# Two MLPs on one core: M1 units moved from ahead of P1 and behind P3 to between P7 and P4, and eight modulation columns read a unit later

## The chip, the cores and the metric

The kernel runs on one core of one Trainium2 chip. The metric is the time of one execution on the device, in microseconds (us), from the first to the last instruction with what the device adds around it. TensorE (PE) does the matmuls, VectorE (DVE) and ScalarE (ACT) the elementwise work. DMAs are issued from three queues: SP's, ScalarE's and GpSimd's (POOL); those on POOL's queue can add what they bring to what lies in the tile (accumulating DMAs).

## The reference

Two decoder layers on 512 tokens of width 1024, all in float32. Each layer has a mixer (pooling in layer 0, a gated unit in layer 1) and an MLP of width 4096; both are modulated by a condition vector. The change touches the MLPs and the modulation:

```python
for i in range(2):
    mod = silu(c) @ ada_w[i] + ada_b[i]              # 6 x 1024 numbers
    sh1, sc1, g1, sh2, sc2, g2 = split(mod, 6)
    h = rmsnorm(x, norm_mix_g[i]) * (1 + sc1) + sh1
    x = x + g1 * mixer(h)                            # pool_mixer, then sgu_mixer
    h = rmsnorm(x, norm_mlp_g[i]) * (1 + sc2) + sh2
    x = x + g2 * (square(relu(h @ mlp_w1[i])) @ mlp_w2[i])
return rmsnorm(x, final_g)
```

## The kernel before

**Precision.** Each operand of a large product is split into a high and a low part: ScalarE writes the high part (`wh`, `oh`; line 176 for weights, line 637 for activations), then VectorE subtracts it from the original and writes the low part (`wl`, `ol`; lines 177 and 638). A product is then three matmuls (`mm3`): low x high, high x low, high x high (lines 187, 188, 190).

**The MLP** (`mlp`) is cut into units that TensorE runs one after the other, in the order of the list `units`. M1 is the first product (h times `mlp_w1`), M2 the second (times `mlp_w2`); the 4096 inner features are cut into four chunks of 1024, with eight feature blocks in each.

- An *f unit* is one block of M1 done directly: 48 matmuls of 256 columns. Layer 0 does chunks 0 and 1 of M1 so (f0 to f7 of chunk 0, f10 to f17 here for chunk 1), layer 1 chunk 0.
- An *s unit* (c, j, m) is one of the seven products (m = 1, 5, 6, 3, 7, 2, 4) of a Strassen-like scheme for half j of chunk c of M1: 24 matmuls of 256 columns. Its finished blocks of `g` are written by VectorE and ScalarE (lines 823 to 831).
- A *p unit* P1, P2, P5, P6, P3, P7, P4 is one of the seven products of such a scheme for one chunk of M2: 24 matmuls of 512 columns into two PSUM banks `pm`. P1, P6, P7 and P4 add into one pair of banks, P5 and P3 and then P2 into another, and after each p unit the pair is added to or subtracted from `y` by VectorE (line 941), or copied by ScalarE the first time (line 944). So P4's first matmul waits until line 941 has read P7's result out of the same pair.
- A *q unit* does the last chunk of M2 directly.

In chunk c of M2 the M1 units of chunk c + 1 are mixed in: `lead` of them ahead of P1, then after P1, P2, P5, P6, P3, P7, P4 as many as `step` says. The order on TensorE is the order written down here. What runs on VectorE, ScalarE, SP and POOL is put in order by a scheduler when the program is built, from the order in which `prep` (operands of later units), `extra` and `run` are called; each engine then keeps to its order.

**Weights.** `raw4` loads 512 KB of weights into one of three buffers (tag `w4`) by a DMA on SP's queue. `wh` and `wl` have five buffers each. P1's weights `bt` (1 MB) have one buffer, which P1, P5, P6 and P4 use in turn, with accumulating DMAs on POOL's queue in between; the next chunk's `bt` is loaded when P4's has been split.

**Modulation.** The layers' modulation vectors are computed on VectorE beside the matmuls: a column of `ada_w` (512 KB, tile `ada`) is loaded on SP's queue (`ada_load`, line 205), then multiplied by the spread condition vector and summed (`ada_tile`, line 215). The two columns of a pair end in `finish_mods` (line 195). In layer 0's MLP `COLUMNS[q]` is the number of the unit in whose turn column q is taken up. Columns 0 to 7 use the three `w4` buffers and are loaded and read in the same turn (`modulation`); columns 8 to 17 have a buffer of their own (`get_gb`) and are read some turns after their load (`modulation_late`), where a copy of one element on ScalarE (line 214), from the latest weight tile, keeps the scheduler from reading earlier.

Of the kernel before, what the change touches and what calls it, by code (L numbers as in the profile page):

```python
# [76 lines left out]
COLUMNS = (0, 1, 2, 3, 5, 9, 12, 14, 19, 22, 25, 28, 31, 34, 37, 40, 44, 48, 57, 58, 58, 58, 58, 58)  # L77
# [4 lines left out]
def decoder_kernel(ctx: ExitStack, tc: tile.TileContext, xtok, vecs, rows, fgrow, ada0, adag, ada1, pool_w, w1s, w1, w1f, w1b, w2, w2e, w_v, w_u, w_o, wsT, lnp, bs, out):  # L82
# [120 lines left out]
    def ada_load(src, get):  # L203
        r = get()
        nc.sync.dma_start(r, src)
        return r

    def ada_tile(i, t, r, late=False):

        b, j = divmod(t, 2)  # L210
        if j == 0:
            pmv[i, b] = sm.tile([P, 2], F32, name="pmv", tag="pmv")
        if late:
            A.activation(pmv[i, b][:, j : j + 1], f32(latest[0])[:, 0:1], AF.Copy)
        V.scalar_tensor_tensor(r, r, 1.0, cb, ALU.mult, ALU.mult, accum_out=pmv[i, b][:, j : j + 1])  # L215
        if j == 1:
            finish_mods(i, b, pmv.pop((i, b)))
# [57 lines left out]
    with (  # L275
# [14 lines left out]
        m = band.rearrange("p n g w -> p (n g) w")  # L290
        G.affine_select(out=m, in_=m, compare_op=ALU.is_ge, fill=0.0, base=0, pattern=[[0, 8], [1, W]], channel_multiplier=-1)
        for g in range(4):
            m = band[:, :, g]
# [297 lines left out]
        for k in range(KD):  # L591
# [16 lines left out]
            fs = [slice(P * f, P * f + P) for f in range(SWEEP)]  # L608
# [18 lines left out]
    ORDER = (1, 5, 6, 3, 7, 2, 4)  # L627
# [15 lines left out]
    def mlp(i, first, extra, last, ending):  # L643
# [3 lines left out]
        with (  # L647
# [339 lines left out]
            units = [("f", (0, f)) for f in range(done, 8)]  # L987
            for c in range(3):
                if c + 1 < FROM[i]:
                    fs, lead, step = [("f", (c + 1, f)) for f in range(8)], 3, (1,) * 7  # L990
                else:
                    fs, lead, step = [("s", (c + 1, j, m)) for j in range(2) for m in ORDER], 3, (1, 2, 3, 2, 2, 1, 0)
                units += fs[0:lead]
                fs = fs[lead:]
                for m, n in zip(ORDER2, step):
                    units.append(("p", (c, m)))
                    units += fs[0:n]
                    fs = fs[n:]
# [97 lines left out]
    def column_at(q):  # L1096
        return (0, 40 + q) if q < 8 else (1, q - 8)

    def modulation(q, get):

        return lambda: ada_tile(*column_at(q), ada_load(ada1[q], get))

    def modulation_late(q, n, get, wait=4):

        r = []
        return [(n, lambda: r.append(ada_load(ada1[q], get))), (n + wait, lambda: ada_tile(*column_at(q), r[0], True))]
# [3 lines left out]
        normed(0, 1, 0)  # L1110


    ex = [(n, modulation(q, get4)) for q, n in enumerate(COLUMNS[:8])]
    for q in range(8, 18):
        ex += modulation_late(q, COLUMNS[q], get_gb, min(4, COLUMNS[q + 1] - COLUMNS[q]))
    ex += [(52, lambda: spread_cols(mods[0][:, c_g(1, 0) : c_g(1, 0) + KD], "gain0"))]
    ex += [(n, modulation(q, get4)) for q, n in enumerate(COLUMNS) if q >= 18]
    mlp(0, first0, ex, gated, ending0)


# [6 lines left out]
    with (  # L1127
# [40 lines left out]
        ex = [modulation(q, get4) for q in range(24, 32)]  # L1168
# [102 lines left out]
    ex = [x for q in range(8) for x in modulation_late(48 + q, 8 + 5 * q, late_gb if q == 0 else get_gb)]  # L1271
    ex += [(58, lambda: spread_cols(mods[1][:, c_g(1, 0) : c_g(1, 0) + KD], "gain1"))]
    mlp(1, first1, ex, last1, lambda: None)


# [78 lines left out]
```

## Time and profile before

| what | value |
|---|---|
| median of 3 runs | 867.54 us (865.52, 867.54, 867.67) |
| profiled execution, its own time | 868.02 us |
| its span, first to last instruction | 866.3 us |
| mean granted TensorE clock | 0.990 |
| TensorE busy | 846.1 us, 98% of the span |
| VectorE busy | 686.6 us, 79% |
| ScalarE busy | 482.5 us, 56% |
| POOL busy | 65.3 us, 8% |

In the span, layer 0's MLP lies between about 90 and 390 us and layer 1's between about 540 and 862 us. A line of a timeline has start and duration in us, the engine, the line of the kernel, the operation, the tiles (out<-in, without buffer numbers), the shapes, and in brackets the idle time of the engine before it with what ended it. "SPq" and "POOLq" are the engines' queues where a DMA is issued.

### The profile page before, as it was taken

The numbers are of one execution on the slowest core, as the hardware profiler recorded it, in microseconds if no ns is written. First come the engines' busy times: TensorE is split into PE (matmuls) and PEld (weight loads), VectorE is DVE, ScalarE is ACT, GpSimd is POOL, SyncE is SP. The second block draws the span as 40 slices with busy tenths as digits, with TensorE's granted clock in tenths as the row PEclk, the third lists the DMA queues.
The fourth block names the chain that finished last, engine by engine and source line by source line (L and its number), as shares of the span: only waits on it lengthen the run. The fifth ranks groups of instructions, "written<-read, shape, count | busy, mean of one in ns | idle before, by whom it ended". The sixth has DMA issues, their size and how long they took to land.

```text
span 866.3 us, 13047 instructions
## 1 busy us (share of the span) xinstructions
PE 846.1 (98%) x5116; PEld 752.4 (87%) x5116; DVE 686.6 (79%) x914; ACT 482.5 (56%) x708; POOL 65.3 (8%) x89
## 2 busy tenths in 40 slices
PE   8999989999999998999999999999999999999996
PEld 7778989989998997888888888999999898999885
DVE  6889697677889888857698866777888988887755
ACT  5286845556656467237433325667766666666521
POOL 3000000010101010010020001000101000010001
PEclk9999989999999999999999999999999999999999
DMA  9969965677879784735755644957789788767302
GB/s 354 417 227 319 327 211 165 193 198 198 200 257 198 234 233 186 254 111 184 242 181 180 198 138 172 333 142 200 153 263 202 252 219 240 203 131 259 122 25 97
DMA packets 43218, 182.34 MB, mean 210 GB/s; under 512 B 4859, under 2 KB 5011, under 8 KB 36118
## 3 DMA queue, kind: packets, MB, share of 16 engines
q1 hardware_dynamic: 35282, 137.72, 44.1%
q0 software_dynamic: 7440, 41.43, 23.8%
q10 hardware_dynamic: 436, 2.37, 0.8%
q8 instruction: 40, 0.66, 0.3%
q14 instruction: 20, 0.16, 0.1%
HBM read 175.19 MB, written 6.30 MB: 210 GB/s over the span
## 4 chain that ended last, share of the span: by engine, by line
PE 72%; DVE 11%; DMA 10%; ACT 4%; issue 3%; SPq 0%; POOLq 0%; POOL 0%; DVEq 0%; ACTq 0%
PE po L187 13%; PE po L190 13%; PE po L188 13%; PE pm L187 10%; PE pm L190 10%; PE pm L188 10%; DMA ada<-in_ada 4%; DVE wl L177 3%; DMA wh<-in_ada 2%; DVE ada L402 1%; ACT wh L176 1%; DVE ada L215 1%; DMA wl<-in_ada 1%; DVE y L941 1%; DMA raw<-in_w1b 1%
## 5 line engine op out<-in xcount | busy, mean ns | idle before, releaser
L187 PE MATMUL po<-hb,wl 128*128 128x256 f32 (+1 forms) x697 | 206.3, 296 | 3.1 <-DVE wl L177 3.0
L188 PE MATMUL po<-hb,wh 128*128 128x256 f32 (+1 forms) x696 | 205.4, 295 | 0.0
L190 PE MATMUL po<-hb,wh 128*128 128x256 f32 (+1 forms) x696 | 205.2, 295 | 0.0
L176 ACT ACTIVATE wh<-raw 128x1024 fp32r<-128x1024 f32 (+1 forms) x122 | 125.8, 1037 | 103.7 <-PE pm L190 36.5
L177 DVE TENSOR_TENSOR wl<-raw,wh 128x1024 fp32r<-128x1024 f32 (+1 forms) x122 | 145.9, 1200 | 44.5 <-ACT wh L176 44.2
L187 PEld LDWEIGHTS po<-hb,wl 128*128 128x128 f32 x697 | 132.1, 190 | 7.9 <-DVE wl L177 3.7
L187 PE MATMUL pm<-wh,ol 128*128 128x512 f32 x336 | 132.6, 395 | 4.5 <-ACT qh L637 3.2
L190 PEld LDWEIGHTS po<-hb,wh 128*128 128x128 f32 x696 | 132.0, 190 | 4.1
L188 PEld LDWEIGHTS po<-hb,wh 128*128 128x128 f32 x696 | 132.1, 190 | 3.9
L190 PE MATMUL pm<-wh,oh 128*128 128x512 f32 (+1 forms) x375 | 132.1, 369 | 0.0
L188 PE MATMUL pm<-wl,oh 128*128 128x512 f32 x336 | 132.0, 393 | 0.0
L215 DVE SCALAR_TENSOR_TENSOR ada<-ada,cb 128x1024 f32<-128x1024 f32 x56 | 68.1, 1219 | 31.3 <-DMA ada<-in_ada 31.0
L190 PEld LDWEIGHTS pm<-wh,oh 128*128 128x128 f32 x375 | 71.1, 190 | 15.2
L187 PEld LDWEIGHTS pm<-wh,ol 128*128 128x128 f32 x336 | 63.8, 190 | 17.1 <-ACT qh L637 3.3
L188 PEld LDWEIGHTS pm<-wl,oh 128*128 128x128 f32 x336 | 63.8, 190 | 11.9
L187 PE MATMUL po<-as,wl 128*128 128x256 f32 x240 | 66.3, 276 | 0.0
L188 PE MATMUL po<-as,wh 128*128 128x256 f32 x240 | 66.3, 276 | 0.0
L190 PE MATMUL po<-as,wh 128*128 128x256 f32 x240 | 66.3, 276 | 0.0
L177 DVE TENSOR_TENSOR wl<-bt,wh 128x1024 fp32r<-128x1024 f32 x48 | 58.3, 1220 | 6.7 <-ACT wh L176 6.5
L177 DVE TENSOR_TENSOR wl<-b,wh 128x1024 fp32r<-128x1024 f32 x36 | 43.7, 1222 | 22.6 <-ACT wh L176 22.5
L176 ACT ACTIVATE wh<-bt 128x1024 fp32r<-128x1024 f32 x48 | 50.2, 1056 | 10.0 <-PE pm L190 2.9
L1050 ACT ACTIVATE tmp<-x 128x512 f32<-128x512 f32 (+1 forms) x25 | 15.3, 611 | 63.9 <-DVE x L1046 57.9
(220 smaller groups left out, 1556.2 us busy)
## 6 DMA issues: line engine op xcount, KB each, us to landing
ada<-in_ada SPq DMA_DIRECT2D x72, 512.0 KB, 4.7
raw<-in_w1b SPq DMA_DIRECT2D x40, 512.0 KB, 5.2
b<-in_w SPq DMA_DIRECT2D x18, 1024.0 KB, 6.0
bt<-in_w POOLq DMA_DIRECT2D x16, 1024.0 KB, 8.5
raw<-in_w1b POOLq DMA_DIRECT2D x20, 512.0 KB, 5.8
raw<-in_w2e SPq DMA_DIRECT2D x16, 512.0 KB, 3.5
bt<-in_w SPq DMA_DIRECT2D x6, 1024.0 KB, 6.5
b<-in_w POOLq DMA_DIRECT2D x6, 1024.0 KB, 9.2
```

The lines of the kernel that those rows point to most:

```text
L176: A.activation(h[:, c], r[:, c], AF.Copy)
L177: V.tensor_tensor(l[:, c], r[:, c], f32(h[:, c]), ALU.subtract)
L187: T.matmul(o[:, c], wl, mh[:, c], start=first and not c.start, stop=False, **kw)
L188: T.matmul(o, wh, ml, start=False, stop=False, **kw)
L190: T.matmul(o[:, c], wh, mh[:, c], start=False, stop=last and c.stop is None, **kw)
L215: V.scalar_tensor_tensor(r, r, 1.0, cb, ALU.mult, ALU.mult, accum_out=pmv[i, b][:, j : j + 1])
L402: V.scalar_tensor_tensor(r, r, 1.0, cb, ALU.mult, ALU.mult, accum_out=out)
L941: V.tensor_tensor(yt, yt, banks[hf], ALU.subtract if minus else ALU.add)
L1050: A.activation(tmp, xt, AF.Square, scale=D**-0.5, accum_out=s[:, len(cs) : len(cs) + 1])
```

## The change

`step` for the directly done chunk gives up the f unit between P3 and P7, so that f17 runs between P7 and P4. For the chunks with s units, `lead` goes from 3 to 2, so P1, P2, P5, P6, P3 and P7 come one s unit earlier, and `step` gains one s unit between P7 and P4 (two instead of one). Columns 0 to 7 are taken with `modulation_late` and a wait of one unit.

```diff
                 if c + 1 < FROM[i]:
-                    fs, lead, step = [("f", (c + 1, f)) for f in range(8)], 3, (1,) * 7
+                    fs, lead, step = [("f", (c + 1, f)) for f in range(8)], 3, (1, 1, 1, 1, 0, 1, 0)
                 else:
-                    fs, lead, step = [("s", (c + 1, j, m)) for j in range(2) for m in ORDER], 3, (1, 2, 3, 2, 2, 1, 0)
+                    fs, lead, step = [("s", (c + 1, j, m)) for j in range(2) for m in ORDER], 2, (1, 2, 3, 2, 2, 2, 0)
...
-    ex = [(n, modulation(q, get4)) for q, n in enumerate(COLUMNS[:8])]
+    ex = [x for q in range(8) for x in modulation_late(q, COLUMNS[q], get4, 1)]
```

The units by number (layer 0) around the first places: before, P3 was unit 12, f17 13, P7 14, P4 15; now P3 is 12, P7 13, f17 14, P4 15. In chunk 1, P1 goes from 19 to 18 and P7 from 34 to 33; P4 stays at 36. All three s-unit chunk changes of layer 1 and both of layer 0 shift alike.

VectorE, at the beginning of layer 0's MLP, before. The `ada` rows of line 215 are the first three column reads, `wl_948` is the low half of f11's weights, `wl_1015` that of f12, `u` and `ol` belong to p units, `as` to the s units:

```order
L721 TENSOR_TENSOR ada_955<-xf_109 128x1024
L215 SCALAR_TENSOR_TENSOR ada_951,pmv_953<-ada_951,cb_101 128x1024
L722 TENSOR_TENSOR xf_109<-xf_109 128x4x256
L723 TENSOR_TENSOR xf_109<-xf_109 128x4x256
L215 SCALAR_TENSOR_TENSOR ada_1018,pmv_953<-ada_1018,cb_101 128x1024
L195 TENSOR_TENSOR mods0_89<-pmv_953,vec_78 128x2
L879 TENSOR_TENSOR u_1427<-g_917 128x1024
L215 SCALAR_TENSOR_TENSOR ada_1092,pmv_1094<-ada_1092,cb_101 128x1024
L177 TENSOR_TENSOR wl_948<-raw_945,wh_947 128x1024
L177 TENSOR_TENSOR wl_1015<-raw_1012,wh_1014 128x1024
```

And now (f12's low half is `wl_1013`):

```order
L721 TENSOR_TENSOR ada_953<-xf_109 128x1024
L722 TENSOR_TENSOR xf_109<-xf_109 128x4x256
L723 TENSOR_TENSOR xf_109<-xf_109 128x4x256
L879 TENSOR_TENSOR u_1432<-g_917 128x1024
L177 TENSOR_TENSOR wl_948<-raw_945,wh_947 128x1024
L177 TENSOR_TENSOR wl_1013<-raw_1010,wh_1012 128x1024
L638 TENSOR_TENSOR as_1022<-xf_109,as_1022 128x1024
L215 SCALAR_TENSOR_TENSOR ada_951,pmv_1016<-ada_951,cb_101 128x1024
L638 TENSOR_TENSOR ol_1080<-g_917,oh_1079 128x1024
L177 TENSOR_TENSOR wl_1084<-bt_1077,wh_1083 128x1024
L177 TENSOR_TENSOR wl_1088<-bt_1077,wh_1087 128x1024
```

The low halves of f11 and f12 moved from behind three column reads to ahead of the first; `wl_1084` and `wl_1088` are P1's.

VectorE around P7's drain (line 941) in chunk 2 of layer 0, before. `wl_3269` and `wl_3273` are P4's weight halves, `g_2988` of line 826 a block of M1, `wl_3336` a weight tile of the q units:

```order
L830 TENSOR_TENSOR g_2988<-g_2988,po_2989 128x2x256
L177 TENSOR_TENSOR wl_3269<-bt_2595,wh_3268 128x1024
L826 TENSOR_TENSOR g_2988<-g_2988,po_3236 128x2x256
L177 TENSOR_TENSOR wl_3273<-bt_2595,wh_3272 128x1024
L177 TENSOR_TENSOR wl_3336<-raw_3333,wh_3335 128x1024
L941 TENSOR_TENSOR y_1255<-y_1255,pm_2719 128x512
L941 TENSOR_TENSOR y_1255<-y_1255,pm_2720 128x512
```

And now, with the bank pair `pm_2691`, `pm_2692`:

```order
L830 TENSOR_TENSOR g_2996<-g_2996,po_2997 128x2x256
L177 TENSOR_TENSOR wl_3276<-bt_2597,wh_3275 128x1024
L177 TENSOR_TENSOR wl_3280<-bt_2597,wh_3279 128x1024
L941 TENSOR_TENSOR y_1259<-y_1259,pm_2691 128x512
L941 TENSOR_TENSOR y_1259<-y_1259,pm_2692 128x512
L177 TENSOR_TENSOR wl_3344<-raw_3341,wh_3343 128x1024
L638 TENSOR_TENSOR ql_3366<-g_2624,qh_3365 128x512
L826 TENSOR_TENSOR g_2996<-g_2996,po_3283 128x2x256
```

The drain moved ahead of the M1 block of line 826 and of the q units' split.

VectorE between two column reads of chunk 1 of layer 0, before:

```order
L215 SCALAR_TENSOR_TENSOR ada_2053,pmv_2050<-ada_2053,cb_101 128x1024
L787 TENSOR_TENSOR raw_1965<-raw_1965,raw_2048 128x1024
L195 TENSOR_TENSOR mods1_90<-pmv_2050,vec_78 128x2
L638 TENSOR_TENSOR ol_2301<-s_2029,oh_2300 128x1024
L199 SCALAR_TENSOR_TENSOR scl10_93<-mods1_90,vec_78 128x1
L177 TENSOR_TENSOR wl_2202<-raw_1965,wh_2201 128x1024
L177 TENSOR_TENSOR wl_2234<-raw_2048,wh_2233 128x1024
L215 SCALAR_TENSOR_TENSOR ada_2172,pmv_2265<-ada_2172,cb_101 128x1024
```

And now:

```order
L215 SCALAR_TENSOR_TENSOR ada_2061,pmv_2058<-ada_2061,cb_101 128x1024
L787 TENSOR_TENSOR raw_1946<-raw_1946,raw_2056 128x1024
L195 TENSOR_TENSOR mods1_90<-pmv_2058,vec_78 128x2
L199 SCALAR_TENSOR_TENSOR scl10_93<-mods1_90,vec_78 128x1
L177 TENSOR_TENSOR wl_2210<-raw_1946,wh_2209 128x1024
L177 TENSOR_TENSOR wl_2276<-b_2268,wh_2275 128x1024
L177 TENSOR_TENSOR wl_2280<-b_2268,wh_2279 128x1024
L941 TENSOR_TENSOR y_1259<-y_1259,pm_1907 128x512
L941 TENSOR_TENSOR y_1259<-y_1259,pm_1908 128x512
L177 TENSOR_TENSOR wl_2284<-raw_2056,wh_2283 128x1024
L215 SCALAR_TENSOR_TENSOR ada_2180,pmv_2289<-ada_2180,cb_101 128x1024
```

Between the two reads there stood six rows, and now nine.

## The prediction

> **What bounds the kernel now.** I read the page first, then the list of waits of TensorE, then a table by stretches of time, and the timeline of each engine around the few places that stood out. The page's span, its busy line of TensorE and the shares of the chain that ended last:
>
> ```profile
> span 866.3 us, 13047 instructions
> PE 846.1 (98%) x5116; PEld 752.4 (87%) x5116; DVE 686.6 (79%) x914; ACT 482.5 (56%) x708; POOL 65.3 (8%) x89
> PE 72%; DVE 11%; DMA 10%; ACT 4%; issue 3%; SPq 0%; POOLq 0%; POOL 0%; DVEq 0%; ACTq 0%
> ```
>
> TensorE is busy for 846.1 of 866.3 us, so a change of order can return only the rest, and whatever TensorE spends at a low clock. The waits of TensorE (total, times, longest):
>
> ```profile
> PE pm L187 <- ACT qh L637: 3.2, 1, 3.2
> PE po L187 <- DVE wl L177: 3.0, 1, 3.0
> PE pm L187 <- DVE y L941: 1.4, 2, 1.0
> ```
>
> These lie in the first MLP. By stretches (length, busy us and instructions of PE, PEld, DVE, ACT, POOL, then granted clock, DMA share, GB/s):
>
> ```profile
> 110.00:120.00 10.00, 7.84 (x45) 7.84 (x46) 10.00 (x12) 3.32 (x5) 0.00 (x0) 0.66 0.64 215
> 340.00:350.00 10.00, 6.84 (x23) 5.46 (x23) 8.33 (x10) 7.55 (x13) 0.00 (x0) 0.66 0.42 128
> 350.00:360.00 10.00, 10.00 (x46) 8.24 (x45) 9.82 (x19) 1.89 (x3) 0.00 (x0) 1.00 0.75 258
> ...
> 540.00:850.00 310.00, 310.00 (x2089) 284.50 (x2089) 246.69 (x270) 193.29 (x255) 24.41 (x31) 1.00 0.70 194
> ```
>
> The second MLP (540 to 850) has no idle time of TensorE to win, only some to lose. In the first, two stretches show a gap and a granted clock of 0.66. So the forecast is a list of four gaps, each with what follows it.
>
> **The first chunk: columns read a unit later.** TensorE stops after f10 and waits for the weights of f11:
>
> ```profile
> 108.90 0.28 PE L190 MATMUL po<-hb,wh 128*128 128x256 f32 x1
> 112.16 0.58 PE L187 MATMUL po<-hb,wl 128*128 128x256 f32 x1 [2.99 <-DVE wl L177]
> 112.54 0.41 PE L188 MATMUL po<-hb,wh 128*128 128x256 f32 x1
> ...
> 118.05 0.28 PE L187 MATMUL po<-hb,wl 128*128 128x256 f32 x1
> 118.17 0.28 PE L188 MATMUL po<-hb,wh 128*128 128x256 f32 x1
> ```
>
> Idle: 2.99 us. Then the steps are 0.21 us instead of 0.113 us until 118.05: 27 matmuls take 5.89 us where 27 x 0.1133 = 3.06 would do, 2.83 lost. Together 5.82 us. What VectorE did meanwhile, and when ScalarE had the high half of f11 (first row) and f12 (second) ready:
>
> ```profile
> 101.06 1.10 ACT L176 ACTIVATE wh<-raw 128x1024 fp32r<-128x1024 f32 x1
> ...
> 102.52 1.10 ACT L176 ACTIVATE wh<-raw 128x1024 fp32r<-128x1024 f32 x1
> ...
> 104.80 1.23 DVE L215 SCALAR_TENSOR_TENSOR ada<-ada,cb 128x1024 f32<-128x1024 f32 x1 [2.40 <-DMA ada<-in_ada]
> ...
> 106.15 1.22 DVE L879 TENSOR_TENSOR u<-g 128x1024 f32<-128x1024 f32 x1
> 109.74 1.23 DVE L215 SCALAR_TENSOR_TENSOR ada<-ada,cb 128x1024 f32<-128x1024 f32 x1 [2.37 <-DMA ada<-in_ada]
> ...
> 110.89 2.36 DVE L177 TENSOR_TENSOR wl<-raw,wh 128x1024 fp32r<-128x1024 f32 x2
> ```
>
> VectorE is in order; it stood before three column reads whose data had not landed, with the low halves of f11 and f12 (wl_948, wl_1015) queued behind. In the changed order both stand ahead of the first column read and wait for ScalarE alone: 102.2 + 1.15 and 103.6 + 1.15, so ready near 103.4 and 104.8, for use at 109.2 and 114.6. The cover is 5.8 us. Next in the queue are as_1022, one column read, ol_1080 and P1's two weight halves, five at 1.15 us, done near 110.6, for P1 at 109.2 + 2 x 5.44 = 120.1 (an f unit is 48 matmuls x 0.1133). So this gap goes whole: 5.82 us. Each of the eight columns holds its buffer of three a unit longer, so SP's next weight load waits longer; the 9.5 us left at P1 is what hides that. The eight added copies of one column on ScalarE cost 0.2 us each, by the rows of those that later columns have already:
>
> ```profile
> L214 ACT ACTIVATE pmv<-wh x18: 183/202/205, 216.0 to 742.6; 128x1 f32<-128x1 f32 x18
> ```
>
> 1.6 us in all, on an engine that is busy for 3.32 of the 10 us from 110: taken as nothing. Without that cover they would cost at most 1.6; the lower bound is nothing, since a copy takes no work off any engine.
>
> **The moved M1 units.** The three other gaps are all in front of the same unit, P4. P4 adds into the two PSUM banks that P7 has just filled, so its first matmul waits until VectorE's line 941 (the drain into y) has read them. The waits' list names ScalarE for the last gap, but the rows show the drain ending just before it:
>
> ```profile
> 186.50 0.47 PE L187 MATMUL pm<-wh,ol 128*128 128x512 f32 x1 [0.40 <-DVE y L941]
> 264.19 0.47 PE L187 MATMUL pm<-wh,ol 128*128 128x512 f32 x1 [0.98 <-DVE y L941]
> 344.18 0.77 PE L187 MATMUL pm<-wh,ol 128*128 128x512 f32 x1 [3.16 <-ACT qh L637]
> 344.74 0.63 PE L188 MATMUL pm<-wl,oh 128*128 128x512 f32 x1
> ...
> 350.21 0.40 PE L190 MATMUL pm<-wh,oh 128*128 128x512 f32 x1
> 350.44 0.40 PE L187 MATMUL pm<-wh,ol 128*128 128x512 f32 x1
> ```
>
> Idle 0.40, 0.98 and 3.16 us. After the last, 14 matmuls from 344.18 to 350.21 take 6.03 us instead of 14 x 0.23 = 3.22 (0.23 is the step after 350.21), 2.81 lost. The end of P7 in chunk 2, and VectorE until its drain:
>
> ```profile
> 337.88 0.40 PE L190 MATMUL pm<-wh,oh 128*128 128x256 f32 x2
> ...
> 338.83 0.68 DVE L826 TENSOR_TENSOR g<-g,po 128x512 f32<-128x512 f32 x1
> 340.09 1.22 DVE L177 TENSOR_TENSOR wl<-bt,wh 128x1024 fp32r<-128x1024 f32 x1 [0.58 <-ACT wh L176]
> 342.21 1.23 DVE L177 TENSOR_TENSOR wl<-raw,wh 128x1024 fp32r<-128x1024 f32 x1 [0.90 <-ACT wh L176]
> 343.36 1.28 DVE L941 TENSOR_TENSOR y<-y,pm 128x512 f32<-128x512 f32 x2
> ```
>
> Now to the cover. Between P7 and P4 stood nothing in chunk 0, and one s unit (24 x 0.1133 = 2.72 us) in chunks 1 and 2; the change puts f17 there (5.44) and two s units (5.44). Chunk 0 needs 0.40 and gets 5.44; chunk 1 needs 0.98 and gets 2.72. Chunk 2 needs 3.16 and gets 2.72 by this alone; but P7 ended near 338.3 and its drain ran only at 343.36, because VectorE had an M1 block (338.83), P4's second weight half (340.09) and a split for the last quarter (342.21) ahead of it, the last two waiting for ScalarE. In the changed order the block and that split stand behind the drain: the block's 0.68, the wait of 0.90 and the split's 343.36 - 342.21 = 1.15 make 2.7 us sooner. 2.72 + 2.7 against 3.16 leaves 2.3 us over. All three go: 0.40 + 0.98 + 3.16 + 2.81 = 7.35 us.
>
> VectorE also gets less late, since the column reads stand farther apart. This one came 9.6 us after its DMA's issue, which lay under accumulating transfers of the POOL queue:
>
> ```profile
> 228.34 0.86 POOL L849 DMA_DIRECT2D bt<-in_w  x1 [5.01 <-DVE wl L177]
> 229.22 9.60 DMA ada<-in_ada
> 238.91 1.23 DVE L215 SCALAR_TENSOR_TENSOR ada<-ada,cb 128x1024 f32<-128x1024 f32 x1 [4.79 <-DMA ada<-in_ada]
> ```
>
> Six rows lay between it and the read before, now nine. I add nothing for it: it widens the cover.
>
> Price on the other side: P1 comes one s unit sooner after P4. Its weights bt have one buffer, free when P4 has split it. In chunk 2 they were split on VectorE by 276.2 and P1 began at 277.92:
>
> ```profile
> 273.88 2.35 DVE L177 TENSOR_TENSOR wl<-bt,wh 128x1024 fp32r<-128x1024 f32 x2
> 277.92 0.39 PE L187 MATMUL pm<-wh,ol 128*128 128x512 f32 x1
> ```
>
> 2.72 sooner is 275.2, 0.17 us after the first half is done (273.88 + 1.15); P1 uses the second half 2.7 us later. With VectorE as late as here that is a cover of nearly nothing; its lateness of 4.79 at 238.91 is what the wider spacing takes away. I cost it at nothing; the bound is a gap at each of the five chunk changes touched, from 0 to 3.16.
>
> The s unit that goes behind P1 takes its block loads (512 KB) on SP's queue with it, behind bt, and its accumulating add on POOL's. By the page's row for bt
>
> ```profile
> bt<-in_w SPq DMA_DIRECT2D x6, 1024.0 KB, 6.5
> ```
>
> such a block could land up to 6.5 us later, for a unit that itself starts 5.44 later: 1.1 us late at worst, nothing where the block is loaded a unit ahead, as here. I take nothing.
>
> No matmul is added or removed, and the number of split last matmuls of a unit is the same.
>
> **Sum** against the profiled execution's 868.02 us (span 866.3; the median of the runs is 867.54, 0.5 lower): 868.02 - 5.82 - 7.35 = 854.85, taken as 854.8 us.
>
> [...] The granted clock falls behind gaps of 2.99 and 3.16 us and behind no shorter one (0.98 and 0.40 us: the next steps are at full rate). [...]
>
> **Rivals.**
> - The slow steps are not the gaps' doing and stay: 868.02 - 2.99 - 0.40 - 0.98 - 3.16 = 860.5. [...] Against it: the rows just named. [...]
> - P4's gaps stay, because VectorE stays as late as it is and the drain keeps its place: 868.02 - 5.82 = 862.2. For it: no work leaves VectorE, busy 10.00 of 10 us around 110 and 9.82 at 350. Against it: the drain's new place.
> - The slower end: P1 now waits for bt. A gap like the two long ones costs about 3.1 + 2.8 = 5.9 us; from the third of the five chunk changes on it outweighs the 13.2 won: three make 854.8 + 17.7 = 872.5. Against it: in the second MLP, where three of the five lie, TensorE shows no gap in 310 us.
> - The change does nothing: columns wait elsewhere, on f13 or P1 instead of f11, and P4's gaps turn up at P1. 868.0.
>
> **Chances.** The forecast 0.78, P4's gaps staying 0.10, the clock 0.05, slower 0.04, nothing 0.03. The 0.3% that a measurement can tell is 2.6 us; so faster is 0.93, same 0.03, slower 0.04. Range: down to 854.8 - 2.5 = 852.3 (the fastest run shown, 865.52, is 2.5 below the profiled one); up to 860.5, the clock's case, which leaves out the 0.17 beyond.
>
> **What would show it.** Right: no wait of TensorE on wl of f11, granted clock 1.00 in every 10 us from 100 to 850, P4's first matmuls without idle time, VectorE idle before column reads for under 1 us each. Wrong: a wait of P1 on wl from bt, a clock of 0.66 anywhere between, a gap at f13, or 0.66 stretches that stay where no gap is.

## The result, and the profile after

The changed kernel took 855.88 us (median of four runs, 854.50 to 856.05), the kernel before 867.61 us beside it: a ratio of 0.9865, with a 95% interval of 0.9845 to 0.9885, or 11.7 us. A second set of runs of the same program gave 855.96 us and a ratio of 0.9885 (0.986 to 0.9911), or 9.5 us. The gain is smaller there because the kernel before took less. Its 53 runs in the later sets show a mean granted clock of 0.992 to 0.998, none the 0.990 of the execution that was profiled, so part of that may be the clock. Forecast were 854.8 us. The profiled execution of the changed kernel took 854.50 us, 13.5 less than that of before; the sum had said 13.2.

The page after: span, TensorE's busy line, and the shares of the chain that ended last.

```profile
span 852.6 us, 13079 instructions
PE 839.5 (98%) x5116; PEld 747.5 (88%) x5116; DVE 686.2 (80%) x914; ACT 484.8 (57%) x716; POOL 65.5 (8%) x89
PE 92%; DMA 4%; ACT 1%; DVE 1%; issue 1%; SPq 0%; POOLq 0%; POOL 0%; DVEq 0%; ACTq 0%
```

VectorE and ScalarE do what they did before (686.2 and 484.8 us), but VectorE's share of the chain fell from 11% to 1%. All of TensorE's waits that are left (total, times, longest):

```profile
PE pg L431 <- DMA ada<-in_adag: 2.9, 2, 1.7
PE px L499 <- ACT xf L503: 1.3, 1, 1.3
PE pc L330 <- DVE edge L297: 1.1, 1, 1.1
PE po L187 <- DVE wl L177: 0.2, 1, 0.2
```

The first three lie in the opening stage, the last at the start of layer 1's MLP. The 3.2, 3.0 and 1.4 us of before are gone. The two stretches that stood at a clock of 0.66, and the second MLP (length, busy us of PE, PEld, DVE, ACT, POOL, then clock, DMA share, GB/s):

```profile
110.00:120.00 10.00, 10.00 (x91) 10.00 (x90) 8.91 (x11) 5.84 (x9) 0.00 (x0) 1.00 0.55 204
340.00:350.00 10.00, 10.00 (x46) 8.26 (x45) 7.85 (x17) 0.74 (x3) 0.00 (x0) 1.00 0.87 294
530.00:840.00 310.00, 310.00 (x2077) 283.97 (x2077) 245.48 (x268) 191.32 (x253) 24.51 (x32) 1.00 0.69 191
```

VectorE at f11 and f12: both low halves now come ahead of the first column read, and that read (106.22) waits for nothing.

```profile
102.48 1.23 DVE L177 TENSOR_TENSOR wl<-raw,wh 128x1024 fp32r<-128x1024 f32 x1 [2.22 <-ACT wh L176]
103.95 1.23 DVE L177 TENSOR_TENSOR wl<-raw,wh 128x1024 fp32r<-128x1024 f32 x1 [0.24 <-ACT wh L176]
...
106.22 1.22 DVE L215 SCALAR_TENSOR_TENSOR ada<-ada,cb 128x1024 f32<-128x1024 f32 x1
```

P7's drain in chunk 2 on VectorE, and P4's first matmul:

```profile
327.65 1.27 DVE L941 TENSOR_TENSOR y<-y,pm 128x512 f32<-128x512 f32 x2
...
333.21 0.39 PE L187 MATMUL pm<-wh,ol 128*128 128x512 f32 x1
```

The first bank is read by 328.33, 4.9 us ahead of P4; the forecast had 2.3 us in hand. One sign of being right did not come: VectorE still stood 2.84 us before a column read (at 350.69), where the forecast had under 1 us for each. No wait of TensorE follows from it.

### The profile page after: what moved, and what is told of

The parts are those of the page before. It is cut to its first block, busy times and chain, and to the rows that moved or that the text cites. A ratio compares the mean times of both kernels' runs of the same rounds, so it can differ in the third digit from the quotient of the medians.

```text
span 852.6 us, 13079 instructions
## 1 busy us (share of the span) xinstructions
PE 839.5 (98%) x5116; PEld 747.5 (88%) x5116; DVE 686.2 (80%) x914; ACT 484.8 (57%) x716; POOL 65.5 (8%) x89
## 4 chain that ended last, share of the span: by engine, by line
PE 92%; DMA 4%; ACT 1%; DVE 1%; issue 1%; SPq 0%; POOLq 0%; POOL 0%; DVEq 0%; ACTq 0%
PE po L187 17%; PE po L190 17%; PE po L188 17%; PE pm L188 12%; PE pm L190 12%; PE pm L187 12%; DMA wh<-in_ada 2%; DMA wl<-in_ada 1%; DMA ada<-in_adag 1%; PE po L1192 1%; ACT sq L315 1%; PE px L1073 1%; PE po L611 0%; PE po L614 0%; PE po L612 0%
## 5 line engine op out<-in xcount | busy, mean ns | idle before, releaser
L187 PE MATMUL pm<-wh,ol 128*128 128x512 f32 x336 | 130.8, 389 | 0.0
```

The lines of the kernel that those rows point to most:

```text
L187: T.matmul(o[:, c], wl, mh[:, c], start=first and not c.start, stop=False, **kw)
```

## The experiments

The ratios are to the runs of the kernel before in the same set (medians of 865.2 to 865.9 us).

### Parts undone: e1, e2, e11

e1 has both new orders of units and the columns read as before.

```diff
-    ex = [x for q in range(8) for x in modulation_late(q, COLUMNS[q], get4, 1)]
+    ex = [(n, modulation(q, get4)) for q, n in enumerate(COLUMNS[:8])]
```

> Both changed orders of units, but the eight columns read in the same turn as before. Theory (each gap has its own cause, and half clock follows a gap of 3 us): the gap before f11 is back, 2.99 idle + 2.83 of slow steps, P4's three gaps stay away: 855.9 + 5.8 = 861.7 us. Rival A (the slow steps are not the gap's doing): only the idle time comes back, 858.9. Rival B (P4's gaps went because the column reads are late and leave VectorE free, not because of the two units between P7 and P4): P4's 0.98 and 3.16 + 2.81 come back too, 867 to 868.

Measured: 860.23 us, ratio 0.9944 (0.9923 to 0.9966). TensorE's only new wait is f11's, and half clock is back behind it (first the wait in the timeline, then two stretches of 3.41 us, columns as above):

```profile
112.98 0.38 PE L187 MATMUL po<-hb,wl 128*128 128x256 f32 x1 [3.82 <-DVE wl L177]
```

```profile
110.42:113.83 3.41, 0.85 (x7) 0.85 (x8) 3.27 (x4) 0.35 (x1) 0.00 (x0) 1.00 0.79 274
113.83:117.25 3.42, 3.42 (x19) 3.42 (x18) 3.42 (x4) 1.98 (x3) 0.00 (x0) 0.50 0.93 344
```

Here and below, half clock is a granted clock of 0.50. Of TensorE's waits the late reads remove f11's and no other: P4 does not wait in this kernel, though the columns are read early. Rivals A and B fall.

e2 puts only chunk 0's order back (`step` of the f units to `(1,) * 7`).

> The changed kernel with the order of chunk 0's f units put back: nothing stands between P7 and P4 in chunk 0. Theory: P4's first matmul there waits 0.4 us for line 941, granted clock stays 1.00: 856.3 us. Rival B (late columns alone make VectorE prompt): no wait, 855.9. Rival C (the moved f17 itself brings more than the wait, by what it does to the order in VectorE): over 857.

Measured: 854.95 us, ratio 0.9883 (0.9861 to 0.9906), too near the changed kernel to time apart, but the trace has the forecast wait to the digit:

```profile
180.79 0.47 PE L187 MATMUL pm<-wh,ol 128*128 128x512 f32 x1 [0.40 <-DVE y L941]
```

e11 changes the s units' order in layer 0 alone.

```diff
-                    ... 2, (1, 2, 3, 2, 2, 2, 0)
+                    ... 3 - (i == 0), ((1, 2, 3, 2, 2, 1, 0), (1, 2, 3, 2, 2, 2, 0))[i == 0]
```

> The changed kernel with lead and step of the s units changed in layer 0 alone, layer 1 as before. The second MLP of the kernel before shows no idle time, so equal to the changed kernel: 855.9 us. Rival (the three chunk changes of layer 1 bring or cost something): off by over 1.5 us.

Measured: 855.04 us, ratio 0.9874 (0.9847 to 0.99). As expected: the three chunk changes of layer 1 bring and cost nothing that can be measured, and no unit of the MLPs waits in the trace.

### Room before P4, or a prompt VectorE: e3, e6, e9, e10

e3 keeps `lead` 2 and leaves one s unit between P7 and P4.

```diff
-                    ... 2, (1, 2, 3, 2, 2, 2, 0)
+                    ... 2, (1, 2, 3, 2, 3, 1, 0)
```

> The changed kernel with one s unit instead of two between P7 and P4 (step 1,2,3,2,3,1,0; lead stays 2): everything but the room before P4. Theory (the bank pair needs the room): gaps before P4 in chunks 1 and 2 of layer 0, 0.98 and 3.16 us with 2.81 of slow steps behind the second, 855.9 + 7.0 = 862.9 us; at most a part of it if VectorE is less late. Rival B (VectorE is prompt once the columns are read late): no gap, 855.9 us.

Measured: 858.16 us, ratio 0.9922 (0.9895 to 0.995). Both gaps are there, the second shorter than before and without half clock:

```profile
257.76 0.47 PE L187 MATMUL pm<-wh,ol 128*128 128x512 f32 x1 [1.10 <-DVE y L941]
...
336.52 0.47 PE L187 MATMUL pm<-wh,ol 128*128 128x512 f32 x1 [1.96 <-ACT qh L637]
```

VectorE waits for no column between 205 and 275 us here. The drain in chunk 1 (256.93) still begins 3.0 us after P7's end, because a block, a column read and two splits stand ahead of it on VectorE; in the changed kernel it stands directly behind P4's two splits and begins as P7 ends (251.01). So with this order the second unit between P7 and P4 is needed, and what it brings is above all the drain's place. e6 keeps that unit and puts P1, P2, P5, P6 and P3 back.

```diff
-                    ... 2, (1, 2, 3, 2, 2, 2, 0)
+                    ... 3, (1, 2, 3, 2, 1, 2, 0)
```

> The changed kernel with lead 3 and step (1,2,3,2,1,2,0): two s units between P7 and P4 as in the change, but P1, P2, P5, P6 and P3 where they were before. Theory (the room between P7 and P4 is what counts, P1's place costs and brings nothing): equal to the changed kernel, 855.9 us. Rival (P1 sooner is what makes P4's weights and VectorE early): drains of P7 late again, a wait before P4 in chunk 1 or 2, 857 to 862 us.

Measured: 860.4 us, ratio 0.9945 (0.9927 to 0.9962): the rival, and a loss of 4.4 us that the theory did not have. VectorE stands before a column again, as it did in the kernel before (4.79 us at 238.91). Behind that P3 waits 0.95 us for a split of its weights, P4 waits in spite of two units of room, and an s unit waits for ScalarE's copy out of its bank (line 823). P4's row names the copy of line 214, but the drain has read the first bank just before it, at 258.27:

```profile
236.29 1.23 DVE L215 SCALAR_TENSOR_TENSOR ada<-ada,cb 128x1024 f32<-128x1024 f32 x1 [5.59 <-DMA ada<-in_ada]
...
257.59 1.28 DVE L941 TENSOR_TENSOR y<-y,pm 128x512 f32<-128x512 f32 x2
258.42 0.47 PE L187 MATMUL pm<-wh,ol 128*128 128x512 f32 x1 [0.54 <-ACT pmv L214]
...
272.14 0.39 PE L187 MATMUL po<-as,wl 128*128 128x256 f32 x1 [2.57 <-ACT g L823]
```

e9 is e6 with columns 8 to 17 a unit later, e10 the kernel before with that edit and no other:

```diff
-COLUMNS = (0, 1, 2, 3, 5, 9, 12, 14, 19, 22, 25, 28, 31, 34, 37, 40, 44, 48, 57, ...
+COLUMNS = (0, 1, 2, 3, 5, 9, 12, 14, 20, 23, 26, 29, 32, 35, 38, 41, 45, 49, 57, ...
```

> The kernel of e6 (lead 3, two s units between P7 and P4, late columns) with columns 8 to 17 taken up one unit later, so that they stand to the p units as with lead 2. Theory V (with lead 3 VectorE stands 4 to 6 us before columns that have not landed, and is late for the drains and the splits behind them; lead 2 took that away): the 5.6 us before the read at 236 go, P4's 0.5, P3's 1.0 and the s unit's 2.6 us with them, 855.9 us. Rival (P1's place itself, through bt or the accumulating DMAs): stays near 860.4 us.

> The kernel before, columns 8 to 17 taken up one unit later, nothing else. Theory V alone (the column waits make P7's drain late): P4's 0.98 us in chunk 1 and 3.16 + 2.81 us in chunk 2 go, the gaps at f11 (5.8) and in chunk 0 (0.4) stay: 865.4 - 7.0 = 858.4 us. Theory T (the room between P7 and P4 and the drain's place behind a block and a split): one unit of room is not enough either way, 864 to 866 us; between the two if both have a part.

Measured: e9 858.54 us, ratio 0.9914 (0.9886 to 0.9942); e10 861.3 us, ratio 0.9946 (0.9925 to 0.9967). In e9 the wait for the column fell to 2.57 us, P4's and P3's went, and of the s unit's wait 1.19 us stayed. TensorE's waits between 100 and 850 us fell from 4.2 to 1.4 us, the median by 1.9 of the 4.4 us: theory V in part. In e10 TensorE waits in the first MLP for these two alone, at f11 and in chunk 0:

```profile
PE po L187 <- DVE wl L177: 3.5, 1, 3.5
PE pm L187 <- DVE y L941: 0.4, 1, 0.4
```

The gaps before P4 in chunks 1 and 2 are gone with the old order of units and 2.72 us of room, as theory V has it. Trace against trace that is 7.0 us (868.02 to 861.00), by the medians 4.6. The drain in chunk 1 still stands behind a split, but it has read the first bank by 262.43, for a P4 at 262.92:

```profile
260.61 1.23 DVE L177 TENSOR_TENSOR wl<-raw,wh 128x1024 fp32r<-128x1024 f32 x1 [1.18 <-ACT wh L176]
261.75 1.28 DVE L941 TENSOR_TENSOR y<-y,pm 128x512 f32<-128x512 f32 x2
```

How late the drain is and how much room it has, from the traces of layer 0 (us). Room is the M1 work between P7 and P4; late is the time from the end of P7's last matmul to the drain's start:

| kernel | room | chunk 1: drain late, P4 waits | chunk 2: drain late, P4 waits |
|---|---|---|---|
| before | 2.72 | 2.9, 0.98 | 5.1, 3.16 |
| e10 | 2.72 | 1.4, 0 | 0.9, 0 |
| e3 | 2.72 | 3.0, 1.10 | 3.9, 1.96 |
| changed, e1 | 5.44 | 0, 0 | 0, 0 |
| e6 | 5.44 | 5.2, 0.54 | 0, 0 |
| e9 | 5.44 | 3.1, 0 | 0, 0 |

P4 waits where the drain is later than the room allows. Two things make the drain late in these runs. One is what stands ahead of it on VectorE (e3). The other is that VectorE comes late to that place: from e6 to e9 the wait for the column in chunk 1 got 3.0 us shorter and the drain 2.1 us less late.

How much of each was at work in the kernel before is not settled, since e10 changed both. In chunk 1 its column wait fell from 4.79 to 1.57 us, but the column read that stood ahead of the drain (261.08) also moved behind it, and that read alone takes more than the 0.98 us that P4 waited. In chunk 2 the longest wait of VectorE ahead of the drain was not for a column (0.96 us at 327.74) but for ScalarE, which waited for a weight tile to land; at the same place in e10 ScalarE waits 0.88 us for its tile and VectorE 0.95 for ScalarE. The kernel before:

```profile
261.08 1.22 DVE L215 SCALAR_TENSOR_TENSOR ada<-ada,cb 128x1024 f32<-128x1024 f32 x1
...
324.46 1.06 ACT L176 ACTIVATE wh<-raw 128x1024 fp32r<-128x1024 f32 x1 [2.82 <-DMA raw<-in_w1b]
325.55 1.23 DVE L177 TENSOR_TENSOR wl<-raw,wh 128x1024 fp32r<-128x1024 f32 x1 [2.89 <-ACT wh L176]
```

### P1 sooner still: e7, e8

```diff
-                    ... 2, (1, 2, 3, 2, 2, 2, 0)
+                    ... 1, (1, 2, 3, 2, 3, 2, 0)        # e7
+                    ... 0, (1, 2, 3, 3, 3, 2, 0)        # e8
```

> The changed kernel with lead 1 and step (1,2,3,2,3,2,0): P1 one s unit (2.72 us) sooner still. In the trace of the changed kernel P1's weights are split 5.6 to 11.9 us ahead of its start, so 2.8 us are left. Theory: equal to the changed kernel, 855.9 us. Rival D (bt's single buffer, the cover of 0.17 us that the prediction worked out): P1 waits at five chunk changes, 0.3 to 3 us each, 858 to 872 us.

> Lead 0 and step (1,2,3,3,3,2,0): P1 directly behind P4. The cover of 5.6 to 6.2 us less 5.44 is 0.1 to 0.8 us at the chunk changes with s units. Theory: no wait or waits of a few tenths, 855.9 to 858 us. Rival D: VectorE splits bt later than that, P1 waits 1 to 3 us at four or five places, half clock behind some of them, 860 to 875 us.

Measured: e7 869.49 us, ratio 1.0046 (1.0026 to 1.0066); e8 872.93 us, ratio 1.0085 (1.0058 to 1.0113). e7 is 0.5% slower than the kernel before, and neither theory had its reason; that 869.49 lies in rival D's range is luck. P1 does not wait; an s unit does, three times (4.17 and 4.10 us in layer 0, 1.01 in layer 1; behind the 4.10 the clock is 0.50 from 304.58 to 307.99):

```profile
PE po L187 <- DVE g L830: 9.3, 3, 4.2
```

With `lead` 1 the s units 7, 2, 4 stand in a row behind P5. Unit 4 adds into the bank that unit 7 filled and waits until line 830 has read it: P7 and P4 over again, with one s unit of room, where the changed kernel has P5 and that unit. In e8 P1 does wait for its weights, at two chunk changes (here the first; 1.16 and 0.77 us at the other, at 736):

```profile
265.38 0.50 PE L187 MATMUL pm<-wh,ol 128*128 128x512 f32 x1 [2.28 <-ACT wh L176]
266.64 0.50 PE L188 MATMUL pm<-wl,oh 128*128 128x512 f32 x1 [0.76 <-DVE wl L177]
```

So rival D is real, but two s units away, not at 0.17 us, and it is the smaller part: s units wait 5.5 us in e8 for the low halves of their weights, 3.10 us of it at 770.94.

### Does the idle time slow the clock: e4

Two places in the kernel before get extra matmuls: into f11's own bank ahead of it, and into a free bank ahead of P4 of chunk 2.

```diff
-                    for k in range(KD):
-
+                    for k in [*range(KD)]:
+                        [T.matmul(po[:, 0:n], H(0, tok[0])[0], H(0, slice(0, n))[0], start=True, stop=True) for _ in range(26 * ((i, c, f, t, k) == (0, 1, 1, 0, 0)))]
...
-                banks = XB if m in IN_X else ZB
+                banks, po = XB if m in IN_X else ZB, [bank("po") for _ in range((i, c, m) == (0, 2, 4))]; [T.matmul(po[0][:, 0:256], H(0, tok[0])[0], H(0, slice(0, 256))[0], start=True, stop=True) for _ in range(27 * len(po))]
```

> The kernel before, with matmuls whose result is overwritten put into its two long gaps: 26 of 256 columns before f11, 27 before P4 of chunk 2 (0.113 us each, 2.9 and 3.1 us). The waits stay, TensorE only does not stand idle in them. Theory (half clock comes from the idle time): both stretches at 0.66 go, 867.6 - 2.83 - 2.81 = 862.0 us. Rival A (the slow steps have another cause): they stay, 867.6 us.

Measured: 865.82 us (861.85 to 868.19), ratio 1.0 (0.9981 to 1.0018). By time this looks like rival A. The trace of one run says otherwise: around both places the clock is whole and TensorE all but never idle.

```profile
109.00:119.00 10.00, 9.66 (x84) 9.46 (x83) 8.68 (x9) 4.94 (x7) 0.00 (x0) 1.00 0.78 288
...
330.00:340.00 10.00, 10.00 (x67) 9.09 (x66) 8.51 (x10) 8.75 (x12) 0.54 (x1) 1.00 0.33 105
340.00:350.00 10.00, 10.00 (x55) 8.63 (x54) 7.95 (x12) 6.18 (x10) 0.00 (x0) 1.00 0.62 179
```

From the start of the first f matmul to the start of TensorE's last one the traced run took 795.04 us, that of before 798.87: 3.8 less, not 5.6. New waits came in (1.07 us at 146.82, 0.34 at f11 and again at 353.61) and the 0.98 us before P4 of chunk 1 went, which makes 0.8 of the 1.8 missing; the rest is open. So is the median: the mean clock of its runs went from 0.993 to 0.999, so some of them may have had slow stretches, and only one was traced. That half clock came with idle time rests on the traces (last section), not on this time.

### The changed kernel again, and the slower steps: e5, e12

> The changed kernel itself, as a measure for the runs of this set: 855.9 us, in its trace no half clock and no wait of TensorE at f11 or P4.

Measured: 855.96 us (853.99 to 856.29), no wait at f11 or P4, clock 1.00. But the traced run took 856.28 us, 1.8 more than the first one traced, and the difference lies in layer 1's f units. 20 us of them, one row each for the first trace, e5 and e12:

```profile
540.00:560.00 20.00, 20.00 (x179) 20.00 (x178) 16.24 (x15) 14.13 (x19) 1.11 (x2) 1.00 0.76 234
```

```profile
540.00:560.00 20.00, 20.00 (x173) 20.00 (x172) 16.46 (x15) 14.03 (x19) 1.01 (x2) 1.00 0.77 237
```

```profile
540.00:560.00 20.00, 20.00 (x173) 20.00 (x172) 16.89 (x16) 13.64 (x19) 0.93 (x1) 1.00 0.76 231
```

Steps of 0.1133 us there, 0.1178 here, at the same granted clock and without a wait. Layer 0's f units begin with a matmul cut in two, and between 100 and 120 us they are at the faster step even in e2 (91 matmuls in each 10 us), whose layer 1 has the slower one (88 in each 10 us from 540 to 560). e12 tries whether that decides it, by cutting two first matmuls of layer 1:

```diff
-  mm3(pos[f][:, c], cut(wf[f], ALL, k), H(k, c), k == 0, k == KD - 1)
+  mm3(pos[f][:, c], cut(wf[f], ALL, k), H(k, c), k == 0, k == KD - 1, half=128 if (hf, f, k) in ((0, 0, 0), (0, 3, 0)) else None)
```

> The changed kernel with the first matmul of layer 1's f units, and the first behind the transposes among them, cut into two of 128 columns, as layer 0's first one is. In some runs the 256-column steps of these units take 0.1178 us instead of 0.1133 (some 350 of them, 1.6 to 2 us), in others not; layer 0's never do. If the cut decides it: always 0.1133, 854.3 us. If not: 0.1178 in some runs as before, 855.9 us, between 854.0 and 856.3.

Measured: 855.55 us (854.24 to 856.89), ratio 0.9879 (0.9854 to 0.9904), and steps of 0.1178 in its trace: the cut does not decide it. No version tried is measurably faster than the changed kernel.

## Why the prediction was right, and where it was not

- **f11, 5.82 us: right, mechanism and size.** Low halves forecast for 103.4 and 104.8 were ready at 103.7 and 105.2. e1 gives back a gap of 3.82 us and 3.41 us at half clock. Trace against trace e1 costs 5.7 us (860.23 against 854.50); by median it lies 4.3 us above e5, and why that is less is open, since only one of its runs was traced.
- **P4 in chunk 0, 0.40 us: right,** shown by e2.
- **P4 in chunks 1 and 2, 6.95 us: right in size, half right in reason.** For chunk 2 the text put the drain ahead of a block and a split, and that is where it came. The step that failed is "chunk 1 needs 0.98 and gets 2.72": it took the drain's lateness as fixed and set room against it. The lateness was 2.9 us and is nothing in the changed kernel, whose added room lies unused. e10 removes both gaps without added room; e6 gives the room and P4 still waits 0.54 us. "I add nothing for it: it widens the cover" named the lateness and made too little of it.
- **What makes VectorE prompt was named too loosely.** "The column reads stand farther apart" does not hold in time: the reads of columns 8 to 17 span 111.4 us before (216.34 to 327.74) and 108.4 now (210.93 to 319.36). What differs is where they stand against the p units. With `lead` 3 VectorE waits up to 4.79 us (before) and 5.59 (e6) for a column between 205 and 345 us, and with the same `lead` and columns a unit later up to 1.57 (e10) and 2.57 (e9). With `lead` 2 it is nothing in the changed kernel and 0.18 in e1, but 2.76 in e3. That such a load is slow because of the accumulating transfers beside it was read off one place (9.60 us from issue to landing at 229.22, before) and not tested.
- **P1 against bt, cover 0.17 us: far too low.** "2.72 sooner is 275.2, 0.17 us after" moved P1 and left the split where it was. But the split of P4's weights, behind which bt is loaded again, moves forward with P1 (20.4 us ahead of it before, 20.1 now), and P1's split follows it 3 us sooner. Before, the first half of P4's weights was split at 257.55 and that of P1's at 273.88 (shown in the prediction). The kernel before, and after it the changed one:

```profile
257.55 1.22 DVE L177 TENSOR_TENSOR wl<-bt,wh 128x1024 fp32r<-128x1024 f32 x1
```

```profile
247.47 1.22 DVE L177 TENSOR_TENSOR wl<-bt,wh 128x1024 fp32r<-128x1024 f32 x1
...
260.79 1.23 DVE L177 TENSOR_TENSOR wl<-bt,wh 128x1024 fp32r<-128x1024 f32 x1 [0.52 <-ACT wh L176]
...
267.58 0.39 PE L187 MATMUL pm<-wh,ol 128*128 128x512 f32 x1
```

 From one to the other were 16.3 us and are 13.3, so P1 has 267.58 - 262.02 = 5.6 us in hand. Costing it at nothing was right by a margin that the text did not have.
- **The copies on ScalarE and the moved loads: nothing, as taken.** No wait of TensorE in the changed kernel names them.
- **The clock's 5.64 us: right here, the reason too coarse.** Both slow stretches went with their gaps. But a gap of 2.99 us had half clock behind it in the kernel before and one of 3.10 us in e8 had not (below), so the length of the gaps does not give the 5.64 us: it is what the profiled execution lost, and what the others lost is not shown. The forecast of 854.8 does not hang on that, since it starts from that execution and takes off what it lost; the gain does. The rival with 860.5 fell by the traces, not by e4's time.
- **The 1.1 us between 854.8 and the median** are not a term of the change: the traced run agrees with the sum within 0.4. The other traced run of this program, e5, has slower steps in layer 1, some 360 x 0.0045 = 1.6 us. That the eight runs that were not traced had them too would explain the median, but is not shown.

## What to carry to other kernels

Where two units share an accumulator, count what stands between them, and ask whether the engine that drains it is late; look for what makes it late (here waits for columns and weights that had not landed, and work that stands ahead of the drain in its engine's order) before giving it more room. When a step is moved, move everything that triggers its loads in the sum as well: a cover worked out with one end fixed is too small. And an order that removes one such pair's wait can make another pair adjacent, as s units 7 and 4 with `lead` 1.

## What the runs showed of the hardware

**In the traces measured here, half clock stood behind stretches of 3.41 us in which TensorE had been idle for 1.99 us or more.** In the kernel before, the granted clock goes to 0.50 at 111.16 and back at 117.98, and again at 343.26 and 350.09; between these places lie 2, 66 and 2 times 3.41 us. Around f11's gap, in steps of 3.41 us:

```profile
107.75:111.16 3.41, 1.42 (x13) 1.22 (x11) 1.42 (x3) 3.04 (x4) 0.00 (x0) 1.00 0.99 394
111.16:114.57 3.41, 2.41 (x11) 2.41 (x12) 3.41 (x4) 0.09 (x1) 0.00 (x0) 0.50 0.78 245
114.57:117.98 3.41, 3.41 (x18) 3.41 (x18) 3.41 (x4) 2.44 (x3) 0.00 (x0) 0.50 0.73 240
117.98:121.40 3.42, 3.42 (x32) 3.42 (x32) 3.42 (x6) 0.76 (x2) 0.00 (x0) 1.00 0.41 125
```

TensorE was busy for 1.42 of the first 3.41 us, and the clock halved at its end, while the gap was still on. It was still 0.50 after the next stretch, busy for 2.41, and 1.00 after the one behind that, wholly busy. e8 has a gap of 3.10 us of which 1.31 and 1.79 us fall into two such stretches, with no half clock behind it, and gaps of 2.28 and 0.76 us with 2.16 us of idle time in one stretch, with half clock behind them:

```profile
263.98:267.39 3.41, 1.25 (x4) 0.85 (x5) 2.03 (x2) 3.12 (x4) 0.00 (x0) 1.00 0.02 8
267.39:270.80 3.41, 3.41 (x9) 2.68 (x9) 3.39 (x5) 3.41 (x5) 0.86 (x1) 0.50 0.47 48
...
765.74:769.15 3.41, 2.10 (x19) 1.91 (x17) 0.00 (x0) 0.57 (x1) 0.00 (x0) 1.00 0.78 278
769.15:772.56 3.41, 1.62 (x14) 1.62 (x15) 2.89 (x4) 3.41 (x5) 0.00 (x0) 1.00 0.17 34
772.56:775.98 3.42, 3.42 (x23) 3.06 (x22) 3.42 (x5) 0.87 (x1) 0.85 (x1) 1.00 0.30 121
```

Stretches of 3.41 us measured in the traces, ahead of TensorE's last matmul, by idle time:

| trace | stretch | TensorE idle in it, us | clock behind it |
|---|---|---|---|
| e7 | 301.17 to 304.58 | 3.41 | 0.50 |
| e10 | 110.00 to 113.41 | 3.17 | 0.50 |
| e1 | 110.42 to 113.83 | 2.56 | 0.50 |
| before | 339.85 to 343.26 | 2.24 | 0.50 |
| e8 | 263.98 to 267.39 | 2.16 | 0.50 |
| before | 107.75 to 111.16 | 1.99 | 0.50 |
| e8 | 769.15 to 772.56 | 1.79 | 1.00 |
| changed | 25.66 to 29.07 | 1.72 | 1.00 |
| e3 | 334.91 to 338.32 | 1.61 | 1.00 |
| e6 | 270.76 to 274.17 | 1.39 | 1.00 |

Gaps of like length cost different amounts in these traces: 1.96 us in e3, 2.57 in e6 and 3.10 in e8 slowed nothing, while 2.99 and 3.16 us in the kernel before had 6.8 us at half clock behind each (2.83 and 2.81 us lost) and 3.82 in e1 had 3.41 us of it, about 1.7 us if half of that counts as lost. How the chip decides it is not shown.

**The same stream of 256-column matmuls ran at one of two steps,** 0.1133 or 0.1178 us, at granted clock 1.00. In layer 1, in the 20 us from 540, it was the slower in five traces (173 matmuls in e2, e5, e11 and e12, 172 in e9) and the faster in those of the kernel before (178) and of the changed one (179). In layer 0, from 110 to 120 us, the traces of the changed kernel and of e2 both have 91 matmuls, the faster step. What sets it is open; in e12 the slower step came with the first matmul split.
